# Seven block products instead of eight in three of eight pairs of the MLP's down product

## The chip, the cores and the metric

The kernel runs on one core of a Trainium2 chip. The metric is the time of one execution on the device in microseconds (us). The core has a matrix engine (TensorE, PE in the profile, with its weight loads as PEld), a vector engine (VectorE, DVE), a scalar engine (ScalarE, ACT), GpSimd (POOL) and SyncE (SP), which here only issues transfers. Each engine takes its instructions in a fixed order.

## The reference, cut to what matters

A two-layer trunk over 256 tokens of width 2048 in float32. Each layer mixes tokens (layer 0 by pooled means, layer 1 by dilated attention with 8 slots in 3 groups of heads) and then runs an MLP of width 8192:

```python
def sqrelu_mlp(x, w_up, w_down):
    h = jax.nn.relu(x @ w_up)
    return (h * h) @ w_down
...
    x = layer_norm(DEEPNORM_ALPHA * x + h, ln_mix_g[i], ln_mix_b[i])
    x = layer_norm(DEEPNORM_ALPHA * x + sqrelu_mlp(x, mlp_w_up[i], mlp_w_down[i]),
                   ln_mlp_g[i], ln_mlp_b[i])
```

## The kernel before, in words

**Split products.** A float32 matrix is held as a high and a low part in float32r. `split_from` (lines 61 to 63) makes them: ScalarE copies to the high part, VectorE subtracts it from the source. A product is three matmuls: high by high, high by low, low by high.

**Weights.** Weights come in chunks of 1024 elements for each of 128 partitions (512 KB), all listed in the order of use. `load` (line 116) fetches a chunk on SyncE's queue into one of 4 raw buffers; `prefetch` (line 129) splits it into one of 8 buffers of high and low parts. `weights()` (line 140) first splits up to 8 chunks ahead of the one in use, counting that one, and then hands it out. TensorE, VectorE and ScalarE run in the order in which the program writes their instructions. So a split that is issued after another operation on VectorE waits for that operation.

**An MLP.** `mlp` (line 520) cuts the 8192 hidden columns into four parts. For each part, `feature_major` forms the up product in blocks of 512 columns (8 chunks a block), hidden features on partitions. After each block `joined` adds two PSUM halves (lines 230, 231), `hidden` applies relu and square on ScalarE (lines 531, 533), and `split_hidden` makes `hH` and `hL`; these are eight pairs of row blocks of 128 for the down product. In the first part of a layer the first two blocks have 256 columns, and after each of the next four blocks `drain` restores a quarter of the residual `xz` on VectorE (lines 352, 353: four operations of 128x512, a multiply and an add for each of two token tiles). Then comes the down product. In three of the four parts (line 563) `token_major` takes 512 columns at a time and both tiles of 128 tokens: 16 row blocks, two tiles, three matmuls of 512 columns, which is 96 matmuls and 8 chunks; VectorE then adds two PSUM banks to `xz` (line 569 or 571). The fourth part goes through `closing`, which also makes the next norm. PSUM has 8 banks that are used in turn.

**Attention.** For each of four pairs of slots, after the third group's values, `transposes` (line 680) turns the weights of one slot with nine transposes, which ScalarE and VectorE split, and `values` multiplies. In the last three pairs `run_later` calls `values` right behind them.

Of the kernel before, what the change touches and what calls it, by code (L numbers as in the profile page):

```python
# [36 lines left out]
RESIDENT = 4  # L37
MLP_PARTS = 4
UP_FIRST = (256, 256, 512, 512, 512)
UP_REST = (512, 512, 512, 512)  # L40
# [6 lines left out]
def trunk(ctx: ExitStack, tc: tile.TileContext, x, pool_w_in, pool_w_group, pool_scale, pool_w_out,  # L47
# [28 lines left out]
    def plan(w, k0, nk, n0, ncols):  # L76
        step = CHUNK // ncols
        for k in range(k0, k0 + nk, step):
            chunks.append((w[:, k:k + step, n0:n0 + ncols], step, ncols))

    def plan_columns(w, k0, nk, n0, widths):
        for ncols in widths:
            plan(w, k0, nk, n0, ncols)
            n0 += ncols

    def plan_mlp(l):
        for c in range(MLP_PARTS):
            plan_columns(w_up[l], 0, KT, c * D, UP_FIRST if c == 0 else UP_REST)
            plan_columns(w_down[l], c * KT, KT, 0, CLOSING if c == MLP_PARTS - 1 else UP_REST)

# [3 lines left out]
    def plan_values(sp):  # L94

        w_v = w_qkv.rearrange("p k (y g n) -> p k y g n", y=3, g=GROUPS)
        for k in range(0, KT, 2):
            chunks.append((w_v[:, k:k + 2, 2, 1:3, sp * 256:(sp + 1) * 256], 2, 512))

# [11 lines left out]
    plan_mlp(1)  # L111

    raws, ready = [], []
    state = {"raw": 0, "split": 0, "used": 0}

    def load(upto):

        while state["raw"] < min(upto, len(chunks)):
            src, step, ncols = chunks[state["raw"]]
            raw = wraw.tile([P, step, ncols], F32, tag="raw", name="raw")  # L120
            if len(src.shape) == 4:
                for j in range(step):
                    nc.sync.dma_start(raw[:, j, :].rearrange("p (g n) -> p g n", g=src.shape[2]), src[:, j])
            else:
                nc.sync.dma_start(raw, src)
            raws.append(raw)
            state["raw"] += 1

    def prefetch(upto):

        while state["split"] < min(upto, len(chunks)):
            load(state["split"] + 1)
            _, step, ncols = chunks[state["split"]]
            hi = wsplit.tile([P, step, ncols], F32R, tag="wh", name="wh")
            lo = wsplit.tile([P, step, ncols], F32R, tag="wl", name="wl")
            split_from(hi, lo, raws.pop(0))
            ready.append((hi, lo))
            state["split"] += 1

    def weights(ahead=SPLITS):  # L140

        prefetch(state["used"] + max(ahead, 1))
        state["used"] += 1
        return ready.pop(0)

    def resident(n):

        prefetch(state["used"] + n)
        state["used"] += n
        return [ready.pop(0) for _ in range(n)]  # L150
# [114 lines left out]
    def tile_products(ps, t, nk, parts, act, start=True, between=()):  # L265

        k = 0
        for i, (hi, lo) in enumerate(parts):
# [7 lines left out]
            k += step  # L276


    class Norm:
        def __init__(self, g, b, cidx, last=None):  # L280
# [58 lines left out]
        def restores(self):  # L339
# [18 lines left out]
            return [lambda n=n: restore(n) for n in range(NG)]  # L358

        def centre(self, t, ns):  # L360
            for n in ns:
                z = xz[:, t, n * 512:(n + 1) * 512]
                nc.vector.scalar_tensor_tensor(z, z, self.mv[t][:, 0:1], self.last[:, 0, n * 512:(n + 1) * 512],
                                               op0=OP.subtract, op1=OP.mult)

        def output(self, t, ns):
            for n in ns:
                sl = slice(n * 512, (n + 1) * 512)
                z = xz[:, t, sl]
                nc.vector.scalar_tensor_tensor(z, z, self.r[t][:, 3:4], self.last[:, 1, sl],  # L370
                                               op0=OP.mult, op1=OP.add)
                nc.sync.dma_start(out[0, t * P:(t + 1) * P, sl], z)

    def closing(nk, act, first, norm, before_last=None):

        held = RESIDENT if norm.last is None else SPLITS
        nres = held * CHUNK // (nk * CLOSING[-1])
# [5 lines left out]
        per = nk * CLOSING[-1] // CHUNK  # L383
        prefetch(state["used"] + SPLITS)
        parts = resident(held)
        def tile_end(t, between=()):
            ps = []
# [13 lines left out]
        norm.moments(0)  # L401
        if norm.last is not None:
            norm.centre(0, [0])
# [32 lines left out]
    def opening(norm, ncols):  # L436
# [7 lines left out]
        for n in range(NG):  # L444
            norm.scaled(1, n)
            norm.features(1, n)
        prefetch(state["used"] + 2)
        tile_products(both[:, 1, :], 1, KT, parts, x_parts, start=False)
# [71 lines left out]
    def mlp(norm_in, norm):  # L520
        with ExitStack() as ph:
            hp = ph.enter_context(tc.tile_pool(name="hp", bufs=8))
            hb = ph.enter_context(tc.tile_pool(name="hb", bufs=2))
            if norm.last is not None:
                for i, v in enumerate((norm.g, norm.b)):
                    nc.gpsimd.dma_start(norm.last[:, i, :], v[None, :].to_broadcast([P, D]))

            def hidden(ps):
# [7 lines left out]
            def split_hidden(q):  # L536
# [3 lines left out]
                return hH, hL  # L540

            for c in range(MLP_PARTS):
                hs = []
                q0 = hidden(opening(norm_in, UP_FIRST[0])) if c == 0 else None
                for ncols in UP_FIRST[1:] if c == 0 else UP_REST:
# [16 lines left out]

                if c < MLP_PARTS - 1:
                    for n in range(NG):
                        ps = token_major(KT, 512, act)
                        for t in range(NT):
                            z = xz[:, t, n * 512:(n + 1) * 512]
                            if c == 0:
                                nc.vector.scalar_tensor_tensor(z, z, ALPHA, ps[t], op0=OP.mult, op1=OP.add)
                            else:  # L570
                                nc.vector.tensor_add(z, z, ps[t])
                else:
                    closing(KT, act, False, norm)
# [6 lines left out]
    with ExitStack() as ph:  # L580
# [44 lines left out]

        def project_values():
            ps = token_major(KT, 512, x_parts)
            hi, lo = value_pair()
# [79 lines left out]
        for sp in range(SLOTS // 2):  # L708
# [42 lines left out]

    fin = ctx.enter_context(tc.tile_pool(name="fin", bufs=1))
    last = fin.tile([P, 2, D], F32, name="last")
    mlp(norm2, Norm(ln_mlp_g[1], ln_mlp_b[1], None, last))


# [21 lines left out]
```

## Time and profile before

| | us |
|---|---|
| median of 3 runs | 2146.39 (2146.17 to 2149.98) |
| the profiled execution | 2146.52 |
| its span from the first to the last instruction | 2144.7 |
| TensorE busy | 2124.7 (99%) |
| VectorE busy | 1283.4 (60%) |
| ScalarE busy | 1052.8 (49%) |

Matmuls are pipelined, so the duration of one (377 ns in the mean at line 245) is longer than the distance from one to the next. The granted TensorE clock is 0.999 of full speed over the span.

### The profile page before, as it was taken

What the parts mean: (1) busy time and instruction counts of PE and PEld (TensorE: products, weight loads), DVE (VectorE), ACT (ScalarE), POOL (GpSimd) and SP (SyncE); (2) the same over time, 40 slices, a digit from 0 to 9 for tenths busy, and PEclk for the clock granted to TensorE, in tenths of its full rate; (3) what the DMA queues carried; (4) which work ended last, traced back from release to release, by engine and by line L of the source; (5) the groups of instructions that cost most, each with busy time, mean ns of one, the idle gap of its engine ahead of it and who ended that gap; (6) DMA issues with size and microseconds to landing.
All of it is one profiled execution on the core that took longest, in us unless ns stands there. A gap on an engine that the chain in (4) does not pass through costs nothing.

```text
span 2144.7 us, 29773 instructions
## 1 busy us (share of the span) xinstructions
PE 2124.7 (99%) x11745; PEld 1845.9 (86%) x11745; DVE 1283.4 (60%) x1558; ACT 1052.8 (49%) x1368; POOL 23.0 (1%) x52
## 2 busy tenths in 40 slices
PE   8999999999999999999999999999999999999998
PEld 7889888888888888898998988888888888888887
DVE  6785756555455555578656565676655555554555
ACT  4563655454355355354545444455545534644541
POOL 1000000000000000001000000000000000000000
PEclk9999999999999999999999999999999999999999
DMA  7565567556655655548555555456665566566562
GB/s 239 204 216 177 169 204 237 175 199 201 191 185 196 194 172 206 194 139 237 173 175 161 176 162 173 164 164 218 209 221 178 201 197 188 176 207 186 181 207 94
DMA packets 256045, 404.67 MB, mean 189 GB/s; under 512 B 13104, under 2 KB 109984, under 8 KB 255648
## 3 DMA queue, kind: packets, MB, share of 16 engines
q1 hardware_dynamic: 253472, 394.31, 56.7%
q0 software_dynamic: 2432, 8.45, 1.9%
q8 instruction: 92, 1.51, 0.3%
q14 instruction: 49, 0.40, 0.1%
HBM read 400.61 MB, written 2.10 MB: 188 GB/s over the span
## 4 chain that ended last, share of the span: by engine, by line
PE 96%; DVE 2%; DMA 1%; ACT 1%; issue 0%; SPq 0%; DVEq 0%; ACTq 0%
PE pt L245 45%; PE pf L202 32%; PE pf L204 16%; PE pf L221 1%; PE pq L658 1%; PE po L697 1%; DMA raw<-in_attn_w_qkv 0%; DVE wl L63 0%; PE ptr L321 0%; DMA xz<-in_x 0%; ACT xv L330 0%; DVE xT L337 0%; DVE vL L63 0%; PE ptr L458 0%; DVE xT L336 0%
## 5 line engine op out<-in xcount | busy, mean ns | idle before, releaser
L63 DVE TENSOR_TENSOR wl<-raw,wh 128x1024 fp32r<-128x1024 f32 x744 | 898.2, 1224 | 621.1 <-ACT wh L62 607.1
L62 ACT ACTIVATE wh<-raw 128x1024 fp32r<-128x1024 f32 x744 | 773.4, 1057 | 805.8 <-PE pt L245 351.4
L202 PE MATMUL pf<-xT,wh 128*128 128x512 f32 x3008 | 947.6, 396 | 0.0
L204 PEld LDWEIGHTS pf<-xT,wl 128*128 128x128 f32 x3008 | 566.0, 188 | 134.0 <-DVE wl L63 0.6
L204 PE MATMUL pf<-xT,wl 128*128 128x256 f32 x3008 | 592.2, 278 | 0.0
L202 PEld LDWEIGHTS pf<-xT,wh 128*128 128x128 f32 x3008 | 459.5, 189 | 0.5
L245 PE MATMUL pt<-wl,hH 128*128 128x512 f32 (+1 forms) x1088 | 407.0, 377 | 0.0
L245 PE MATMUL pt<-wh,hH 128*128 128x512 f32 (+1 forms) x1088 | 407.0, 377 | 0.0
L245 PE MATMUL pt<-wh,hL 128*128 128x512 f32 (+1 forms) x1088 | 398.2, 377 | 0.0
L245 PEld LDWEIGHTS pt<-wl,hH 128*128 128x128 f32 x1088 | 204.8, 188 | 37.6 <-DVE wl L63 0.4
L245 PEld LDWEIGHTS pt<-wh,hH 128*128 128x128 f32 x1088 | 204.8, 188 | 37.5
L245 PEld LDWEIGHTS pt<-wh,hL 128*128 128x128 f32 x1088 | 199.6, 188 | 37.1
L245 PE MATMUL pt<-wh,xT 128*128 128x256 f32 (+1 forms) x704 | 156.4, 314 | 1.9 <-DVE xT L336 1.5
L245 PEld LDWEIGHTS pt<-wh,xT 128*128 128x128 f32 x704 | 117.2, 191 | 10.6 <-DVE xT L336 3.1
L63 DVE TENSOR_TENSOR hL<-q,hH 128x512 fp32r<-128x512 f32 x62 | 42.9, 693 | 125.6 <-ACT hH L62 125.6
L245 PE MATMUL pt<-wl,xT 128*128 128x256 f32 (+1 forms) x352 | 106.7, 312 | 0.0
L230 ACT ACTIVATE low<-pf 128x256 f32<-128x256 f32 x188 | 61.3, 377 | 69.6 <-PE pf L204 62.7
L245 PE MATMUL pt<-wh,pT 128*128 128x512 f32 (+1 forms) x320 | 82.6, 347 | 0.0
L231 DVE TENSOR_TENSOR u<-pf,low 128x256 f32<-128x256 f32 x172 | 64.7, 418 | 26.0 <-ACT low L230 26.0
L245 PEld LDWEIGHTS pt<-wl,xT 128*128 128x128 f32 x352 | 67.2, 191 | 3.6
L531 ACT ACTIVATE r<-u 128x512 f32<-128x512 f32 x62 | 39.2, 632 | 51.0 <-DVE u L231 51.0
L245 PEld LDWEIGHTS pt<-wh,pT 128*128 128x128 f32 x320 | 56.1, 189 | 7.5
(126 smaller groups left out, 1001.8 us busy)
## 6 DMA issues: line engine op xcount, KB each, us to landing
raw<-in_mlp_w_up SPq DMA_DIRECT2D x256, 512.0 KB, 4.4
raw<-in_mlp_w_down SPq DMA_DIRECT2D x256, 512.0 KB, 4.5
raw<-in_attn_w_qkv SPq DMA_DIRECT2D x120, 512.0 KB, 4.3
raw<-in_pool_w_in SPq DMA_DIRECT2D x32, 512.0 KB, 5.4
raw<-in_pool_w_out SPq DMA_DIRECT2D x32, 512.0 KB, 4.7
raw<-in_attn_w_qkv SPq DMA_DIRECT2D x48, 256.0 KB, 3.3
raw<-in_attn_w_out SPq DMA_DIRECT2D x16, 512.0 KB, 4.4
raw<-in_pool_w_group SPq DMA_DIRECT2D x8, 512.0 KB, 5.0
```

Of the source, the lines that this page charges most:

```text
L62: nc.scalar.activation(hi, src, AF.Copy)
L63: nc.vector.tensor_sub(lo, src, hi.bitcast(F32))
L202: nc.tensor.matmul(ps[b], hi[:, j, sl], a, start=(k == 0), stop=False, skip_group_check=True)
L204: nc.tensor.matmul(ps[b][:, 0, :], lo[:, j, sl], a[:, 0, :], start=False, stop=(k == nk - 1), skip_group_check=True)
L221: nc.tensor.matmul(ps[b // 2][:, b % 2, :], w[:, j, sl], a[:, part, :], start=(k == 0 and i == 0 and b % 2 == 0), stop=(k == nk - 1 and i ...
L230: nc.scalar.activation(low, p[:, 1, :], AF.Copy)
L231: nc.vector.tensor_add(out[:, b, :], p[:, 0, :], low)
L245: nc.tensor.matmul(ps, a[:, sl], u, start=(start and k == 0 and i == 0), stop=(k == nk - 1 and i == 2), skip_group_check=True)
L531: nc.scalar.activation(r, ps, AF.Relu)
L658: nc.tensor.matmul(pq[:, t, :], q[u][:, b, sl], k[v][:, b, :], start=(i == 0), stop=(i == 2))
L697: nc.tensor.matmul(po, v[:, st, b * P:(b + 1) * P], p[:, g, sl], start=(i == 0), stop=(i == 3 * 2 * GROUPS - 1))
```

## The change

In the first three parts of each MLP the down product is formed for 1024 columns at a time by `mixed_group`. Of eight pairs of row blocks, taken in the order 1, 0, 3, 2, 5, 4, 6, 7, the pairs 1, 3 and 5 are treated as a product of 2x2 blocks (two token tiles by two row blocks, times two row blocks by two column halves) and formed by seven block products of sums and differences; the other pairs by eight. All eight banks of PSUM collect the products, and `sums` (8 VectorE operations) and four closing additions bring them into `xz`. The weight sums are made on VectorE in float32 and then split (`split_seven`), the sums of the hidden blocks likewise (`split_seven_left`). A seven-product chunk is two raw buffers and four split buffers, and `prefetch` counts it as four units of eight. Besides: plain chunks of these parts hold one row block by 1024 columns; in attention `transposes` moves ahead of the last value chunk in the last three pairs; the gain and bias rows of the last norm go into raw buffers on SyncE's queue at the last `closing`, and no longer through GpSimd's queue into a buffer of their own.

```diff
+MIX = (1, 0, 3, 2, 5, 4, 6, 7)
+SEVEN = (1, 3, 5)
+WIDE = 1024
...
+    def plan_mixed(w, k0, n0):
+        for i in MIX:
+            k = k0 + 2 * i
+            if i in SEVEN:
+                chunks.append((w[:, k:k + 2, n0:n0 + WIDE], 2, WIDE, 4))
+            else:
+                plan(w, k, 2, n0, WIDE)
...
+    def split_seven(a, b):
+        left, right = a[:, :512], a[:, 512:]
+        t = state["diff"].tile([P, 4, 512], F32, tag="t", name="t")
+        nc.vector.tensor_sub(t[:, 0], right, left)
+        nc.vector.tensor_sub(t[:, 1], b[:, :512], left)
+        nc.vector.tensor_add(t[:, 2], b[:, :512], t[:, 0])
+        nc.vector.tensor_sub(t[:, 3], b[:, 512:], t[:, 2])
+        parts = []
+        for src in (right[:, None, :], t[:, 0:2], b.rearrange("p (i n) -> p i n", i=2), t[:, 2:4]):
+            parts.append(split_buffers([P, 2, 512]))
+            split_from(parts[-1][0][:, :src.shape[1]], parts[-1][1][:, :src.shape[1]], src)
...
     def prefetch(upto):
-        while state["split"] < min(upto, len(chunks)):
+        while state["split"] < len(chunks) and begins[state["split"] + 1] <= upto:
...
+    def lookahead(n):
+        prefetch(begins[state["used"]] + n)
...
+    def mixed_group(act, left_factors, z, first):
+        names = ("P1", "P5", "P7", "P6", "P2", "P3", "P4", "P0")
+        ps = {name: bank([P, 512], "pt") for name in names}
...
+        def sums():
+            one, two, three = (tmp.tile([P, 512], F32, tag="xv", name="us", bufs=3) for _ in range(3))
+            nc.scalar.activation(one, ps["P1"], AF.Copy)
+            nc.vector.tensor_add(two, ps["P6"], one)
+            add(0, 1, ps["P1"], True)
+            nc.vector.tensor_add(three, ps["P7"], two)
+            nc.vector.tensor_add(two, ps["P5"], two)
+            add(1, 1, three, True)
+            nc.vector.tensor_add(three, ps["P5"], three)
+            add(0, 0, two, True)
+            add(1, 0, three, True)
+
+        last_seven = max(MIX.index(i) for i in SEVEN)
+        for n, i in enumerate(MIX):
+            a, b = 2 * i, 2 * i + 1
+            if i in SEVEN:
+                w, f = weights(), left_factors[i]
+                for name, left, right in (("P1", tokens(a, 0), "B11"), ("P5", f(0), "T1"), ("P7", f(2), "T3"),
+                                          ("P6", f(1), "T2"), ("P2", tokens(b, 0), "B21"), ("P3", f(3), "B22"),
+                                          ("P4", tokens(b, 1), "T4")):
+                    product(name, left, w[right], n == last_seven and name in ("P1", "P5", "P7", "P6"))
+            else:
+                for k in (a, b):
+                    hi, lo = weights()
+                    for name, t, h in (("P2", 0, 1), ("P3", 0, 0), ("P4", 1, 1), ("P0", 1, 0)):
+                        sl = slice(h * 512, (h + 1) * 512)
+                        product(name, tokens(k, t), (hi[:, 0, sl], lo[:, 0, sl]), n == len(MIX) - 1 and k == b)
+            if n == last_seven + 1:
+                sums()
+        add(0, 1, ps["P2"])
+        add(0, 0, ps["P3"])
+        add(1, 1, ps["P4"])
+        add(1, 0, ps["P0"])
...
+            def split_seven_left(q):
+                (a11, a21), (a12, a22) = ((q[:, i, :P], q[:, i, P:]) for i in range(2))
+                d = hb.tile([P, 4, P], F32, tag="r", name="d")
...
+                split_from(dH, dL, d)
...
-                        hs.append(split_hidden(hidden(u)))
+                        q = hidden(u)
+                        if c < MLP_PARTS - 1 and len(hs) in SEVEN:
+                            left_factors[len(hs)] = split_seven_left(q)
+                        hs.append(split_hidden(q))
...
-            vs.extend([project_value(pair, 1)] if sp == 0 else project_values())
-            transposes(sc[js[0]])
+            if sp == 0:
+                vs.append(project_value(pair, 1))
+                transposes(sc[js[0]])
+            else:
+                vs.extend(project_values(lambda: transposes(sc[js[0]])))
```

## Rows read from the trace of the kernel before

**Rows 1.** Page, part 1: busy us (share of the span), instructions.
```profile
PE 2124.7 (99%) x11745; PEld 1845.9 (86%) x11745; DVE 1283.4 (60%) x1558; ACT 1052.8 (49%) x1368; POOL 23.0 (1%) x52
```
**Rows 2.** Busy time by stretch: two down products, the up product between; header names columns.
```profile
core 0: us, PE busy (x) PEld busy (x) DVE busy (x) ACT busy (x) POOL busy (x), PEclk, DMA share, GB/s
308.50:395.80 87.30, 87.30 (x386) 72.00 (x385) 52.71 (x53) 42.66 (x46) 1.06 (x2) 1.00 0.72 238
395.80:485.00 89.20, 89.20 (x514) 77.88 (x513) 48.06 (x54) 48.24 (x64) 0.00 (x0) 1.00 0.57 187
485.00:572.05 87.05, 87.05 (x385) 72.10 (x385) 45.36 (x45) 37.84 (x40) 0.00 (x0) 1.00 0.62 196
```
**Rows 3.** Chain that ended last: three of six down products; start, length.
```profile
308.50 87.33 PE pt L245 x384
...
485.00 87.05 PE pt L245 x384
...
1517.13 87.11 PE pt L245 x384
```
**Rows 4.** Instruction groups by shape: busy us, mean ns, then idle before them.
```profile
L63 DVE TENSOR_TENSOR wl<-raw,wh 128x1024 fp32r<-128x1024 f32 x744 | 898.2, 1224 | 621.1 <-ACT wh L62 607.1 <-PE pf L204 6.5 <-PE pf L202 2.0
L62 ACT ACTIVATE wh<-raw 128x1024 fp32r<-128x1024 f32 x744 | 773.4, 1057 | 805.8 <-PE pt L245 351.4 <-PE pf L202 198.2 <-DMA raw<-in_mlp_w_down 111.3
...
L63 DVE TENSOR_TENSOR hL<-q,hH 128x512 fp32r<-128x512 f32 x62 | 42.9, 693 | 125.6 <-ACT hH L62 125.6
...
L661 DVE SCALAR_TENSOR_TENSOR sc<-dist,pq 128x128 f32<-128x128 f32 x24 | 6.7, 280 | 0.0
```
**Rows 5.** VectorE's timeline, first parts' down products: start, length (merged), idle before.
```profile
302.13 4.62 DVE L63 TENSOR_TENSOR wl<-raw,wh 128x1024 fp32r<-128x1024 f32 x4
311.96 5.19 DVE L63 TENSOR_TENSOR wl<-raw,wh 128x1024 fp32r<-128x1024 f32 x4 [5.20 <-ACT wh L62]
317.06 0.75 DVE L231 TENSOR_TENSOR u<-pf,low 128x256 f32<-128x256 f32 x2
...
323.23 0.69 DVE L63 TENSOR_TENSOR hL<-q,hH 128x512 fp32r<-128x512 f32 x1 [2.03 <-ACT hH L62]
323.83 0.69 DVE L352 TENSOR_TENSOR xz<-xz,gb 128x512 f32<-128x512 f32 x1
...
326.49 4.62 DVE L63 TENSOR_TENSOR wl<-raw,wh 128x1024 fp32r<-128x1024 f32 x4
...
1534.86 4.63 DVE L63 TENSOR_TENSOR wl<-raw,wh 128x1024 fp32r<-128x1024 f32 x4
```
**Rows 6.** TensorE's timeline at the eighth chunk of that product.
```profile
327.41 0.39 PE L245 MATMUL pt<-wh,hH 128*128 128x512 f32 x1
327.76 0.50 PE L245 MATMUL pt<-wl,hH 128*128 128x512 f32 x1
```
**Rows 7.** VectorE's timeline, second part's down product: its last hidden block, then weights.
```profile
484.64 0.76 DVE L231 TENSOR_TENSOR u<-pf,low 128x256 f32<-128x256 f32 x2 [0.30 <-ACT low L230]
...
490.80 0.69 DVE L63 TENSOR_TENSOR hL<-q,hH 128x512 fp32r<-128x512 f32 x1 [2.02 <-ACT hH L62]
491.75 4.63 DVE L63 TENSOR_TENSOR wl<-raw,wh 128x1024 fp32r<-128x1024 f32 x4 [0.26 <-ACT wh L62]
...
506.53 1.28 DVE L571 TENSOR_TENSOR xz<-xz,pt 128x512 f32<-128x512 f32 x2
```
**Rows 8.** Page, part 6: transfers, KB each, median us from issue to landing.
```profile
raw<-in_mlp_w_down SPq DMA_DIRECT2D x256, 512.0 KB, 4.5
```
**Rows 9.** TensorE's timeline in attention: the last transpose, the third value matmul.
```profile
1147.89 0.27 PE L685 MATMUL pp<-ident,sc 128*128 128x128 f32 x1
...
1149.06 0.39 PE L697 MATMUL po<-PTL,vH 128*128 128x256 f32 x1 [0.30 <-DVE PTL L63]
```
**Rows 10.** Busy time by stretch at the end; columns as in rows 2.
```profile
2134.00:2135.00 1.00, 0.15 (x2) 0.00 (x0) 0.78 (x2) 0.00 (x0) 0.00 (x0) 1.00 0.00 0
...
2139.00:2140.00 1.00, 0.00 (x0) 0.00 (x0) 1.00 (x3) 0.00 (x0) 0.00 (x0) 0.61 0.00 0
```

More of the change, by code (lines that the diff above doesn't have):

```diff
@@ L111, in trunk @@
     plan_mlp(1)
+    begins = [0]
+    for c in chunks:
+        begins.append(begins[-1] + c[3])
     raws, ready = [], []
@@ L118, in load @@
         while state["raw"] < min(upto, len(chunks)):
-            src, step, ncols = chunks[state["raw"]]
-            raw = wraw.tile([P, step, ncols], F32, tag="raw", name="raw")
-            if len(src.shape) == 4:
+            src, step, ncols, units = chunks[state["raw"]]
+            if units > 1:
+                raw = [wraw.tile([P, ncols], F32, tag="raw", name="raw") for _ in range(step)]
                 for j in range(step):
-                    nc.sync.dma_start(raw[:, j, :].rearrange("p (g n) -> p g n", g=src.shape[2]), src[:, j])
+                    nc.sync.dma_start(raw[j], src[:, j])
@@ L124, in load, with split_buffers @@
             else:
-                nc.sync.dma_start(raw, src)
+                raw = wraw.tile([P, step, ncols], F32, tag="raw", name="raw")
+                if len(src.shape) == 4:
+                    for j in range(step):
+                        nc.sync.dma_start(raw[:, j, :].rearrange("p (g n) -> p g n", g=src.shape[2]), src[:, j])
+                else:
+                    nc.sync.dma_start(raw, src)
             raws.append(raw)
             state["raw"] += 1
+    def split_buffers(shape):
+        return [wsplit.tile(shape, F32R, tag="w" + x, name="w" + x) for x in "hl"]
@@ new lines, in split_seven @@
+    def split_seven(a, b):
[9 more added lines that the diff above has]
+            split_from(parts[-1][0][:, :src.shape[1]], parts[-1][1][:, :src.shape[1]], src)
+        (one, diff, low, sums) = parts
+        return {name: (h[:, i], l[:, i]) for name, (h, l), i in (
+            ("B11", one, 0), ("T1", diff, 0), ("T3", diff, 1), ("B22", low, 0), ("B21", low, 1),
+            ("T2", sums, 0), ("T4", sums, 1))}
@@ L129, in prefetch @@
     def prefetch(upto):
-        while state["split"] < min(upto, len(chunks)):
+        while state["split"] < len(chunks) and begins[state["split"] + 1] <= upto:
             load(state["split"] + 1)
[L133 to L137, printed above, removed]
+            _, step, ncols, units = chunks[state["split"]]
+            raw = raws.pop(0)
+            if units > 1:
+                ready.append(split_seven(*raw))
+            else:
+                hi, lo = split_buffers([P, step, ncols])
+                split_from(hi, lo, raw)
+                ready.append((hi, lo))
@@ L146, in resident @@
     def resident(n):
[L148 removed]
+        lookahead(n)
         state["used"] += n
@@ L358, in restores, with rows_of_last, row @@
             return [lambda n=n: restore(n) for n in range(NG)]
+        def rows_of_last(self):
+            self.rows = []
+            for v in (self.g, self.b):
+                for n0 in range(0, D, CHUNK):
+                    self.rows.append(wraw.tile([P, CHUNK], F32, tag="raw", name="row"))
+                    nc.sync.dma_start(self.rows[-1], v[None, n0:n0 + CHUNK].to_broadcast([P, CHUNK]))
+        def row(self, i, n):
+            return self.rows[i * D // CHUNK + n // 2][:, n % 2 * 512:(n % 2 + 1) * 512]
         def centre(self, t, ns):
@@ L374, in closing @@
     def closing(nk, act, first, norm, before_last=None):
-        held = RESIDENT if norm.last is None else SPLITS
+        held = RESIDENT if not norm.last else SPLITS
         nres = held * CHUNK // (nk * CLOSING[-1])
@@ L401, in closing @@
         norm.moments(0)
-        if norm.last is not None:
+        if norm.last:
             norm.centre(0, [0])
@@ L563, in mlp @@
                 if c < MLP_PARTS - 1:
[L564 to L571, printed above, removed]
+                    for n0 in range(0, D, WIDE):
+                        mixed_group(act, left_factors,
+                                    lambda t, h: xz[:, t, n0 + h * 512:n0 + (h + 1) * 512], c == 0)
                 else:
```

61 lines of the change are left out of this document (43 added, 18 removed).

## The prediction

> **What bounds the kernel now.** I read the page's busy shares first: TensorE 99% of a span of 2144.7 us, VectorE 60% [rows 1]. That is an average, so next came the busy time by stage. The six stretches that change are the three down products of each layer that end in a plain addition: 384 matmuls in 87.05 us [rows 3], 0.2267 us each from start to start, with no gap. In such a stretch VectorE is busy 45.4 us, or 52.7 us in the first of a layer [rows 2]. The forecast hangs on VectorE's timeline where a down product begins, and that is where the reader should look: just after that start VectorE spends 6.9 us on the last hidden block (317.06 to 323.92), 2.7 us on restoring the residual (323.83 to 326.49), and only then splits weights again [rows 5]. The eighth weight chunk of the down product is the first of that burst. It is ready at about 327.72 (326.49 and one 1.23 us subtraction) and TensorE, which wants it at 308.50 + 7 x 2.72 = 327.5, starts its second product at 327.76 instead of 327.64 [rows 6]. So at this place the first part of a layer has no reserve at all; in the other layer the same burst starts at 1534.86 [rows 5] and the product at 1517.13 [rows 3], 17.7 us on instead of 18.0, again with almost nothing spare.
>
> **The change on TensorE.** A pair of row blocks was 24 matmuls for 1024 columns and becomes 21. Three pairs, two column halves, six parts: 3 x 3 x 2 x 6 = 108 matmuls fewer, all on the path, 108 x 0.2267 = 24.5 us saved. A seven-product pair then takes 4.76 us, a plain one 5.44, a part 83.0 instead of 87.05.
>
> **The change on VectorE.** A 1024-wide weight subtraction lasts 1.22 us alone and follows the one before by (4.62 - 1.23)/3 = 1.13 us [rows 4, 5]; two 512-wide additions from PSUM take 1.28 us together, 0.6 us apart [rows 7]; four 512-wide ones in SBUF take the 2.66 us of the restore [rows 5]. A seven-product chunk was two subtractions (2.3 us). It becomes four 512-wide sums (2.66) and splits of 0.6 + 3 x 1.13 (4.0): 6.7 us. ScalarE's part, 3.5 x 1.06 = 3.7 us [rows 4], lies beside it. The sums of block products add eight 512-wide operations to each of 12 groups, 5.3 us each. By stage: six such chunks add 26 us to a part and two sums 10.6, so VectorE's 45.4 becomes 82 against TensorE's 83.0, and the 52.7 of a first part becomes 90. VectorE sets the pace there. Each left factor (pairs 1, 3, 5) adds four 128-wide operations, at 0.28 us by the nearest row, and a 512-wide subtraction of 0.69 [rows 4]: 1.8 us in the chain of its hidden block. Nothing covers it, for VectorE waits there for ScalarE, which waits for it.
>
> [...]
>
> **How a down product begins.** Eight units of split weights are kept ahead. Before, seven chunks (19 us of TensorE) were split ahead of the last hidden block. Now a seven-product chunk takes four units, and only the first of them and two plain chunks are ahead: 4.76 + 5.44 = 10.2 us. The second one, B, comes behind the hidden block in VectorE's program order.
>
> *Second and third parts* (four of the six). The hidden block ends at 491.49 - 485.00 = 6.5 us [rows 3, 7]. B's last split is ready at 6.5 + 6.7 = 13.2; TensorE wants it at 10.2 + 2.27 (P1, P5, P7 and one matmul) = 12.5: a stall of 0.7. From there VectorE has, up to the first of the closing additions that free PSUM banks, 2.3 (two chunks), 6.7, 6.8 (six chunks), 5.3 (sums), 6.7 (the next group's first chunk), 2.3, 0.65: it ends at 44.0 without waits, and at up to 47 if weights that land 4.5 us after their issue [rows 8] arrive late at two places, since VectorE now holds the four raw buffers longer. TensorE wants that bank at 41.5 + 0.7 + 2.7 = 44.9. That stall is 0 to 2 us; I take 1.0. Sum 1.75, bounds 0 and 4, four times: +7.0.
>
> *First parts* (two). Three left factors put the chain, which paces VectorE between bursts, 5.5 us later: the burst of 302.13 begins at 307.6. Its chunk was needed at 308.50 - 2.79 = 305.7 (a chunk of the up product is 89.2/32 [rows 2]), so TensorE stalls 3 us already there. Then 1.2 (that chunk), 6.7 (A) and 2.3: hidden block at 317.8, restore at 324.7, B's sums from 327.3, its last split at 334.0. TensorE finishes B 2.5 us later, at 336.5, against 308.50 + 4.76 + 5.44 + 4.76 = 323.5 with no stall: 13.0 us. With 0 to 1.6 for the bank (0.8 taken) 13.8, twice: +27.6. Bounds: 7 if the left factors cost nothing (B 5.5 us earlier, no late bank), 16 if the loads add to it.
>
> **Other edits.** In three of four head pairs transposes move ahead of the last value chunk, a chunk that covers their splits. TensorE now waits some 1149.06 - (1147.89 + 0.11) - 2 x 0.12 = 0.8 us there [rows 9], 0.11 and 0.12 being half the pace of 0.2267 for matmuls of at most 256 columns; behind them the value splits still come late, so I take 0.5 gained, bounds 0 and 0.8: -1.5. Plain chunks of one row block and 1024 columns move the same bytes and feed the same 12 matmuls: 0. The last norm's rows go from two transfers on GpSimd's queue to four on SyncE's, 512 KB each, behind the last weights and ahead of the output's. They are wanted only after the first tile's closing products, 48 x 0.2267 = 10.9 us, which cover 4.5 us of landing [rows 8]; uncovered they would cost those 4.5.
>
> **Sum.** -24.5 - 1.5 + 7.0 + 27.6 = +8.6. The profiled execution took 2146.5 us (span 2144.7 and 1.8 around it), beside a median of 2146.4: 2155.1 us.
>
> **Rivals.**
> (1) *VectorE keeps ahead.* If the splits of B were done before they are wanted, only the saving is left: 2146.5 - 26 = 2120.5, faster. For it: the share of VectorE over the whole span stays near 71%. Against: order on VectorE is the program's, the reserve of 10.2 us is shorter than hidden block plus B (13.2), and the row at 327.76 shows no slack.
> (2) *The left factors are absorbed.* Fewer chunks are split before the hidden block now, so the wait for loads inside the burst (306.7 to 312.0 [rows 5]) goes. If this also takes up the 5.5 us, a first part stalls 7.5 us: -26 + 15 + 7 = -4, 2142.5 us, on the edge of faster. The sign turns at a stall of (26 - 7)/2 = 9.5 us in a first part. Against: that wait is already left out of my walk.
> [...]
>
> **How the numbers follow.** A measurement here can tell about 0.2%, 4.3 us. My forecast has 0.55, its own range 2148 to 2163 us; of it 0.38 lies above 2150.7 and 0.17 within 0.2%. Rival 1 has 0.12, rival 2 0.16 (half faster, half same), rival 3 0.17 (slower). Together: faster 0.20, same 0.25, slower 0.55. From 2134 to 2168 about 0.8 is held: rival 1 and half of rival 3 lie outside.
>
> **What would show it.** Right: in 308 to 400 and 1517 to 1610 the stretch of down products is longer than 87 us, about 97, with VectorE busy some nine tenths and TensorE waiting for it at the start; in the other four it is 84 to 86 us, with first waits some 13 us in; matmuls fall by 108, and VectorE's busy time rises by some 250 us (36 x 4.4 + 12 x 5.3 + 18 x 1.8). Wrong: first parts of 83 to 90 us, or the four others over 88. The step that I trust least is the 13 us of a first part, since one order of work on VectorE makes it.

## The result, and the profile after

The changed kernel took 2170.48 us in the median of four runs (2169.10 to 2171.14), the kernel before 2146.28 in four runs beside it: a ratio of 1.0108 (95% interval 1.0090 to 1.0125; it is worked out from the single runs, the two medians alone give 1.0113). It is slower, as forecast, but by 23.5 us between the two profiled executions (2146.52 and 2169.97) where 8.6 were said, and above the range of 2148 to 2163. The page of the profile, part 1, and then the busy time by stretch of the six down products, with the columns of [rows 2]:

```profile
PE 2118.3 (98%) x11637; PEld 1831.6 (84%) x11637; DVE 1511.0 (70%) x1960; ACT 1117.5 (52%) x1470; POOL 22.0 (1%) x50
```
```profile
311.71:405.79 94.08, 86.32 (x368) 69.70 (x368) 81.54 (x98) 51.68 (x60) 1.06 (x2) 0.98 0.62 206
494.95:580.06 85.11, 83.57 (x369) 68.52 (x367) 73.28 (x89) 48.27 (x56) 0.00 (x0) 1.00 0.58 193
669.22:755.57 86.35, 83.61 (x368) 68.47 (x367) 73.95 (x89) 48.65 (x56) 0.00 (x0) 1.00 0.56 190
1528.07:1625.30 97.23, 89.62 (x368) 71.23 (x367) 83.59 (x101) 52.87 (x61) 0.00 (x0) 0.95 0.59 198
1714.47:1802.51 88.04, 85.30 (x368) 69.57 (x367) 76.00 (x91) 48.60 (x56) 0.00 (x0) 0.98 0.58 192
1891.67:1980.12 88.45, 85.45 (x368) 69.59 (x367) 74.85 (x90) 48.49 (x56) 0.00 (x0) 0.98 0.56 187
```

The 108 matmuls are gone and VectorE has 227.6 us more to do, against [rows 1]. With no stall each stretch would be 83.0 us. The four stretches of second and third parts are 2.1, 3.4, 5.0 and 5.5 us longer, 16.0 in all where 7.0 were said; those of layer 1 are the ones with a mean clock of 0.98, and both are over the 88 us that the prediction named as a sign against it. The first parts begin late as well: from the second up block (256 columns) to the end of the down product layer 0 takes 176.1 us (229.66 to 405.79) and layer 1 179.8 (1445.53 to 1625.30), where 165.8 and 165.6 less 4.1 saved were possible: 14.4 and 18.3 us lost, 32.7 in all where 27.6 were said.

What TensorE waited for, over the whole span (us in total, times, longest):

```profile
PE pt L343 <- DVE xz L355: 11.0, 6, 2.1
PE pt L343 <- DVE wl L67: 8.4, 11, 2.2
PE pt L343 <- DVE u L285: 5.9, 4, 1.9
...
PE pf L258 <- DVE wl L67: 5.3, 3, 2.9
```

The first row is one wait in each of the six parts, in the middle: in the second group's first chunk the fifth product wants a bank that a closing addition (line 355) has not yet read. The other three belong to the first parts for the most part: the late up chunk (line 258), the banks of the last up block, which VectorE adds late (line 285), and B, the second seven-product chunk of a group (A is the first). In the second and third parts the wait for B is 0.6 us each, where 0.7 was said. VectorE's timeline at the first down product, beside [rows 5]:

```profile
306.71 1.22 DVE L67 TENSOR_TENSOR wl<-raw,wh 128x1024 fp32r<-128x1024 f32 x1
...
316.65 0.75 DVE L285 TENSOR_TENSOR u<-pf,low 128x256 f32<-128x256 f32 x2
...
323.42 0.68 DVE L465 TENSOR_TENSOR xz<-xz,gb 128x512 f32<-128x512 f32 x1
...
326.08 0.69 DVE L163 TENSOR_TENSOR t<-raw 128x512 f32<-128x512 f32 x1
...
331.48 1.22 DVE L67 TENSOR_TENSOR wl<-t,wh 128x1024 fp32r<-128x1024 f32 x1
```

The walk of the forecast put these at 307.6 (the late chunk), 317.8 (hidden block), 324.7 (restore), 327.3 (B's sums) and 334.0 (B's last split ready; here 332.7). It held within 1.3 us.

What the walk did not hold is the clock. Busy time in 1 us stretches around the bank wait of layer 1's second part; the granted clock is the third column from the end:

```profile
1758.00:1760.00 2.00, 1.87 (x8) 1.05 (x7) 2.00 (x2) 1.35 (x2) 0.00 (x0) 1.00 0.54 182
1760.00:1761.00 1.00, 0.00 (x0) 0.00 (x0) 1.00 (x2) 0.00 (x0) 0.00 (x0) 1.00 0.61 234
1761.00:1762.00 1.00, 0.00 (x0) 0.00 (x1) 1.00 (x3) 0.00 (x0) 0.00 (x0) 1.00 0.70 188
1762.00:1763.00 1.00, 1.00 (x4) 0.86 (x5) 1.00 (x2) 0.00 (x0) 0.00 (x0) 0.97 0.88 299
1763.00:1764.00 1.00, 1.00 (x4) 0.71 (x4) 1.00 (x3) 0.00 (x0) 0.00 (x0) 0.50 0.59 152
1764.00:1765.00 1.00, 1.00 (x4) 0.81 (x3) 1.00 (x3) 0.00 (x0) 0.00 (x0) 0.50 0.69 233
1765.00:1766.00 1.00, 1.00 (x4) 0.81 (x3) 0.97 (x2) 0.94 (x1) 0.00 (x0) 0.50 0.46 188
1766.00:1767.00 1.00, 1.00 (x5) 0.79 (x4) 1.00 (x3) 1.00 (x3) 0.00 (x0) 0.82 0.00 0
```

TensorE stands still for 2 us and runs for 1, and then the granted clock reads 0.50 for 3 us. The column lacks 0.03 + 3 x 0.50 + 0.18, so 1.7 us of full clock are lost. There are seven such falls of 1.7 us each, two at the start of each first part and three at bank waits, all of these in layer 1.

### The profile page after: what moved, and what is told of

The parts are those of the page before. It is cut to its first block, busy times and chain, and to the rows that moved or that the text cites. A ratio compares the mean times of both kernels' runs of the same rounds, so it can differ in the third digit from the quotient of the medians.

```text
span 2168.2 us, 30026 instructions
## 1 busy us (share of the span) xinstructions
PE 2118.3 (98%) x11637; PEld 1831.6 (84%) x11637; DVE 1511.0 (70%) x1960; ACT 1117.5 (52%) x1470; POOL 22.0 (1%) x50
## 4 chain that ended last, share of the span: by engine, by line
PE 75%; DVE 14%; DMA 5%; ACT 3%; issue 2%; DVEq 0%; SPq 0%; ACTq 0%
PE pf L256 28%; PE pt L299 21%; PE pf L258 14%; PE pt L343 11%; DVE wl L67 6%; DMA raw<-in_mlp_w_down 3%; DMA raw<-in_mlp_w_up 1%; ACT wh L66 1%; DMA raw<-in_pool_w_in 1%; PE pq L793 1%; PE po L832 1%; DVE xz L355 1%; DVE u L285 1%; DVE win L624 1%; DVE t L166 1%
## 5 line engine op out<-in xcount | busy, mean ns | idle before, releaser
L67 DVE TENSOR_TENSOR wl<-raw,wh 128x1024 fp32r<-128x1024 f32 (+1 forms) x744 | 875.4, 1196 | 402.4 <-ACT wh L66 397.2
L66 ACT ACTIVATE wh<-raw 128x1024 fp32r<-128x1024 f32 (+1 forms) x744 | 757.7, 1035 | 602.1 <-PE pf L256 162.5
L343 PE MATMUL pt<-wh,hH 128*128 128x512 f32 x588 | 232.0, 395 | 16.9 <-DVE xz L355 11.0
L343 PE MATMUL pt<-wl,hH 128*128 128x512 f32 x588 | 231.1, 393 | 4.7 <-DVE wl L67 4.7
L343 PE MATMUL pt<-wh,hL 128*128 128x512 f32 x588 | 230.5, 392 | 0.0
L343 PEld LDWEIGHTS pt<-wh,hH 128*128 128x128 f32 x588 | 111.6, 190 | 44.4 <-DVE xz L355 13.6
L343 PEld LDWEIGHTS pt<-wl,hH 128*128 128x128 f32 x588 | 111.7, 190 | 28.5 <-DVE wl L67 5.9
L299 PE MATMUL pt<-wh,hH 128*128 128x512 f32 (+1 forms) x320 | 107.9, 347 | 0.0
L299 PE MATMUL pt<-wl,hH 128*128 128x512 f32 (+1 forms) x320 | 107.8, 347 | 0.0
L299 PE MATMUL pt<-wh,hL 128*128 128x512 f32 (+1 forms) x320 | 99.2, 347 | 0.0
```

The costliest lines, as they stand in the source:

```text
L66: nc.scalar.activation(hi, src, AF.Copy)
L67: nc.vector.tensor_sub(lo, src, hi.bitcast(F32))
L299: nc.tensor.matmul(ps, a[:, sl], u, start=(start and k == 0 and i == 0), stop=(k == nk - 1 and i == 2), skip_group_check=True)
L343: nc.tensor.matmul(ps[name], a[u], w[v], start=(name not in begun), stop=(last and i == 2), skip_group_check=True)
```

## The experiments

Ratios are to the kernel before, whose median beside them was 2147.2 to 2147.4 us; differences between experiments are those of their medians. The changed kernel was not run again beside them, and the kernel before was 1.0 us faster beside it than beside them, so a difference of a microsecond or two from the changed kernel says nothing.

**Which part pays: e1 and e2.** Seven products in the second and third parts alone, and in none.

```diff
-    def plan_mixed(w, k0, n0):
+    def plan_mixed(w, k0, n0, seven):
...
-            if i in SEVEN:
+            if i in seven:
...
-plan_mixed(w_down[l], c * KT, n0)
+plan_mixed(w_down[l], c * KT, n0, SEVEN if c in PARTS else ())   # e1: PARTS = (1, 2); e2: ()
```


> Seven-product pairs only in the second and third parts; the first part of each layer goes back to eight products per pair (in 1024-column groups, without left factors). Theory A (order: too little weight split ahead of the last hidden block, worst where the residual is restored too): the first parts cost +10.3 and +14.2 us by the stage marks of the two traces, so this gives 2170.5 - 24.5 = 2146 us, and the other four parts stay at 85 to 88.5 us each. Rival B (VectorE is simply full and its total work is what is lost, wherever it lies): two of six parts' work taken off, one third of the loss and of the saving, some 2162 us.

> Eight products in every pair, with all that came beside the seven products kept (1024-column groups and chunks, transposes ahead of the last value chunk, last norm's rows through raw buffers). Theory A: 2145 to 2146 us, half a microsecond to one and a half below the kernel before. Rival D (the wider chunks or the rows of the last norm carry a part of the loss): above 2150.

e1: 2146.94 us (ratio 0.9996, 0.9986 to 1.0006). e2: 2145.31 (0.9990, 0.9981 to 0.9999). Both are what the theory of order expected. The other edits of the change cost nothing; second and third parts break even, and the first parts make the loss.

**The bank wait: e3 and e7.** In plain chunks of a group the lookahead is cut so that the closing additions come ahead of the splits of the two plain chunks behind the next A. e7 does this with seven products in the second and third parts alone.

```diff
+        limit = begins[state["used"]] + 22 + 4
...
-                    hi, lo = weights()
+                    hi, lo = weights(min(SPLITS, limit - begins[state["used"]]))
```


> All work kept; only the order on VectorE and ScalarE changes at the end of each group: the four closing additions, which free PSUM banks, come ahead of the splits of the two plain chunks behind the next group's first seven-product chunk. Theory A: the bank waits at the middle of each part (1 to 2 us, six times) go, and with them three stretches of lower clock of 1.7 us each: 2155 to 2161 us. Rival B: VectorE has the same work, 2168 to 2171. Rival C (the clock costs nothing, TensorE would have waited anyway): 2159 to 2163.

> The first and the third of these runs together: seven products in second and third parts only, closing additions ahead of the splits. Theory A: each of four parts gains 4.1 us on TensorE and waits 0.7 us for the second seven-product chunk, so 2146 - 13 = 2132 to 2134 us, faster than both kernels. Rival B: 2144 to 2148.

e3: 2157.36 (1.0046, 1.0031 to 1.0061), 13.1 us less than the changed kernel; no wait for those additions is left among its waits. e7: 2138.08 (0.9957, 0.9942 to 0.9972), faster than both kernels, though each of its four parts gains 2.2 us on e1 where 3 and more were expected: a miss, between the ranges of both theories.

**The clock: e4 and e9.** Eight products with a zero left factor, which change no sum, go ahead of the first product that meets the bank wait, so that TensorE has work there; e9 adds such filler at three places at the start of the first parts.

```diff
+                    if second and n == 0 and name == "P2":
+                        idle_products(ps["P1"], w["B11"][0], 8)
+                    if first and not second and n == 0 and name in ("P2", "P4"):   # e9 as well
+                        idle_products(ps["P1"], w["B11"][0], 6)
+                    if first and not second and n == 2 and name == "P1":             # e9 as well
+                        idle_products(ps["P0"], last_w, 8)
...
```


> Work added to TensorE alone: in the second group of each part eight matmuls with a zero left factor (1.8 us, they add nothing) stand ahead of the product that waits for a bank, so TensorE is busy where it waited. Theory A: the clock no longer falls behind that wait (three of six parts, 1.7 us each) and the filler fits into the wait: 2164 to 2167 us. Rival C (the lower clock costs nothing because VectorE is behind anyway): 2169 to 2172.

> The same filler, and in the first part of each layer filler in the first group too: six zero matmuls ahead of each of two bank waits in the first seven-product chunk, eight ahead of the second one's first product. There VectorE is still behind when the clock falls, so theory A has little left to gain: 0 to 3 us below the run with filler at the middle alone, 2162 to 2167. If the clock's whole 1.7 us were lost at each fall there, 5 us below it: 2160.

e4: 2164.07 (1.0078, 1.0065 to 1.0091). Eight more matmuls at six places made the kernel 6.4 us faster; by the two traces all of it was gained in layer 1, where the three falls had been. The same bank wait in e4, columns as before:

```profile
1760.00:1761.00 1.00, 1.00 (x6) 0.78 (x5) 1.00 (x3) 0.00 (x0) 0.00 (x0) 1.00 0.65 234
...
1763.00:1764.00 1.00, 1.00 (x6) 0.84 (x5) 1.00 (x3) 1.00 (x3) 0.00 (x0) 1.00 0.07 16
```

So the falls at the bank waits are real losses: three of 1.7 us are 5.1 of the 6.4. e9: 2163.82 (1.0076, 1.0062 to 1.0090). Filling the starts as well brings nothing, although the full clock lost there shrinks from 8.5 us in e4 to 3.4: there TensorE has to wait for VectorE anyway, at either clock.

**The start of a first part: e8, e5, e5b.** e8 forms the left factors once in a layer and uses them for all pairs and parts of it, so that 16 of the 18 formations are left out (not 17, as the expectations say) and the product is no longer that of the reference: e8, and e15 and e16 below, tell of the time alone. e5 moves the restoring operation that stands between the last hidden block and B behind the sums of the first group; e5b does that on e3.

```diff
-                            left_factors[len(hs)] = split_seven_left(q)
+                            left_factors[len(hs)] = state["left"] = state.get("left") or split_seven_left(q)   # e8
...
-                    drain()                                  # e5, e5b
+                    if not (c == 0 and len(hs) == 8):
+                        drain()
...
                 sums()
+                drain()
```


> The left factors (sums of hidden blocks and their split) are formed once and used again in all later pairs, so 17 of 18 formations are left out and the products are not those of the reference. Theory A: in each first part the chain of hidden blocks and restores comes 3 x 1.83 = 5.5 us earlier (one formation less in the first layer), the other parts hardly change; with one fall of the clock less in the first layer 2157 to 2161 us. The rival of the prediction that the 5.5 us are absorbed by a shorter wait for loads: 2168 to 2171.

> The changed kernel (2170.5 us) with the restoring operation alone moved behind the sums of the first group. The queue theory gives up to 5 us and perhaps a fall of the clock less: 2164 to 2168 us. The theory of a full VectorE gives no change, since the bank wait between the groups takes back what B gained: 2169 to 2172 us.

> e3 (2157.4 us) with the restoring operation that stands between the last hidden block and B in the two first parts taken to the place behind the sums of the first group. If what makes B late is VectorE's queue ahead of it, this brings up to 2.7 us in each first part: 2152 to 2155 us. If VectorE is short of time over the whole first part, the moved operation makes a later split or sum late by as much: 2156 to 2159 us.

All three miss what the theory of a late queue expected. e8: 2165.75 (1.0087, 1.0074 to 1.0101), a gain of 4.7 us, between its two theories. e5: 2174.19 (1.0128, 1.0113 to 1.0144), above both of its ranges, and e5b: 2157.23 (1.0048, 1.0034 to 1.0061), where a VectorE short of time was expected: no gain. In e5 B's sums begin 2.2 us sooner, at 323.88, and the next chunk's then wait 0.65 us for a weight transfer.

**Another engine, another order: e10, e11, e12.** e10 puts the four weight sums of a chunk on GpSimd, on e3. e11 starts each group with a plain pair, so that more of TensorE's work lies ahead of A and B, and gives the banks out to match; e12 is e11 in the second and third parts alone.

```diff
-        nc.vector.tensor_sub(t[:, 0], right, left)
+        nc.gpsimd.tensor_sub(t[:, 0], right, left)      # e10: and the three sums below it
...
-MIX = (1, 0, 3, 2, 5, 4, 6, 7)
+MIX = (0, 1, 2, 3, 4, 5, 6, 7)                          # e11, e12
...
-        names = ("P1", "P5", "P7", "P6", "P2", "P3", "P4", "P0")
+        names = ("P2", "P3", "P4", "P0", "P1", "P5", "P7", "P6")
+        if second:
+            names = names[4:] + names[:4]
```


> Closing additions first, and the four float32 sums of each seven-product chunk made on GpSimd instead of VectorE (36 x 2.6 us less on VectorE). Theory A: the second chunk of each part is split some 2.6 us earlier if GpSimd makes the sums while VectorE is in the hidden block, so the wait of 0.7 us in four parts goes and each first part gains 3 to 5 us: 2142 to 2150 us, against 2157.4 with closing additions first alone. If GpSimd takes longer than some 6 us for the four, or slows VectorE: 2157 or more.

> All three parts keep seven products, and the closing additions keep their place of e3 (2157.4 us). The order inside each group becomes plain pair, A, plain, B, plain, C, plain, plain, and the banks are named so that the first plain products of a first group take banks that the last up block does not hold, and those of a second group the banks that the sums have freed. No instruction is added or removed. Theory of the reserve: at the entry of a first part the eight split buffers then cover 5.4 + 4.8 + 5.4 = 15.6 us of TensorE's work in place of 10.2, so the wait for B shrinks by about 5 us in each of the two first parts, and the bank wait between the groups goes too, since a plain pair lies ahead of A: 2143 to 2148 us. Rival: VectorE is full from the last up blocks to the end of a first part, so that a different order only moves the wait from B to C or to the end: 2155 to 2158 us.

> The order and the banks of e11 with seven products in the second and third parts alone, as in e7 (2138.1 us). In those parts VectorE has time, so what is left of waits there should be the order's: the reserve theory gives 2132 to 2136 us. The rival, that what e7 still lacked of 3.4 us a part is VectorE's own time in these parts, gives 2137 to 2139 us.

e10: 2163.40 (1.0072, 1.0058 to 1.0086), 6.0 us slower than e3: the gain that was hoped for is missed, and what the expectation named for a slow GpSimd came. Groups of instructions of e10, GpSimd's and VectorE's (busy, mean ns, idle before):

```profile
L164 POOL TENSOR_TENSOR t<-raw 128x512 f32<-128x512 f32 x36 | 64.5, 1793 | 16.5 <-DMA raw<-in_mlp_w_down 16.4
...
L163 POOL TENSOR_TENSOR t<-raw 128x512 f32<-128x512 f32 x36 | 61.5, 1707 | 620.4 <-DMA raw<-in_mlp_w_down 521.1 <-DVE wl L67 83.5 <-ACT hH L66 15.9
```
```profile
L67 DVE TENSOR_TENSOR wl<-raw,wh 128x512 fp32r<-128x512 f32 x36 | 40.7, 1131 | 0.2 <-ACT wh L66 0.2
```

A sum takes 1.6 to 1.8 us there, and the 512-wide subtraction that VectorE makes of such a chunk 1131 ns in the mean, against 685 in the changed kernel. Single instructions of e10 show that it depends on what lies beside them (start, length):

```profile
360.78 0.68 DVE L67 TENSOR_TENSOR wl<-raw,wh 128x512 fp32r<-128x512 f32 x1
...
538.18 2.47 DVE L356 TENSOR_TENSOR xz<-xz,pt 128x512 f32<-128x512 f32 x4
538.52 1.30 POOL L163 TENSOR_TENSOR t<-raw 128x512 f32<-128x512 f32 x1 [5.43 <-DMA raw<-in_mlp_w_down]
...
542.89 2.28 POOL L165 TENSOR_TENSOR t<-raw,t 128x512 f32<-128x512 f32 x1
543.94 1.78 DVE L67 TENSOR_TENSOR wl<-raw,wh 128x512 fp32r<-128x512 f32 x1
```

With no GpSimd sum beside it the subtraction takes 0.68 us, beside one 1.78; four closing additions, whose second input is a PSUM bank, take 2.47 us together, 0.6 us apart, also beside one (676 ns each in the mean of e10, 678 in the changed kernel).

e11: 2172.73 (1.0117, 1.0103 to 1.0131), 15.4 us slower than e3; both theories miss. e12: 2138.12 (0.9958, 0.9946 to 0.9971), as e7 and in the range of its rival: its down products do shrink to 83.0 to 83.5 us, but the next up block then waits 1.3 us in the mean for a bank that the sums hold. VectorE's timeline in e11 shows what the order ran into:

```profile
310.54 0.69 DVE L163 TENSOR_TENSOR t<-raw 128x512 f32<-128x512 f32 x1
316.23 0.69 DVE L164 TENSOR_TENSOR t<-raw 128x512 f32<-128x512 f32 x1 [5.01 <-DMA raw<-in_mlp_w_down]
```

VectorE, late already, stands for 5.0 us inside A for A's second raw row. The four raw buffers were taken, so that row could not be fetched sooner.

**Less work ahead of a first part: e13, e14, e15.** Restoring operations one by one earlier, in the up blocks: on the changed kernel, on e3, and on e3 with the left factors formed once.

```diff
                         hs.append(split_hidden(q))
+                        if c == 0 and len(ps) == 4 and i == 0:
+                            drain()
                     drain()
```


> The changed kernel (2170.5 us) with the four restoring operations of each layer put one up block pair after another, so that the last two stand before the last up block instead of inside it and behind it. The same instructions, 5.4 us of VectorE's work per first part moved to a stretch in which VectorE is busy for two thirds of the time. If VectorE's work between the last up block and the end of the first part sets the time, each first part gains 5 us and a part of its clock falls: 2156 to 2161 us. If the loads into the raw buffers set it, only the wait for the late up chunk (2.0 and 2.9 us) goes, or is given back: 2166 to 2171 us.

> The same edit on e3 (2157.4 us), where the closing additions stand ahead of the splits for later plain chunks. VectorE's work as the cause: 2144 to 2149 us. Loads as the cause: 2153 to 2158 us.

> The kernel of e14 in which a layer forms its left factors for one block pair alone and uses them for all (17 of 18 formings of 5.4 us on VectorE left out in every two layers, so the product is not the reference's). With the restoring operations and the left factors both gone from the entry, the theory of VectorE's work expects first parts that cost no more than plain ones or gain like the others, 2135 to 2142 us, against 2144 to 2149 of e14. The theory of the loads expects 2150 us or more here too.

e13: 2169.07 (1.0102, 1.0086 to 1.0118). e14: 2157.93 (1.0049, 1.0037 to 1.0062). e15: 2156.28 (1.0039, 1.0026 to 1.0052). All three lie where the theory of the loads put them. None gains more than 1.7 us over its base, so with four raw buffers VectorE's work at that place is not by itself what sets the time. (By its timeline e14 takes one restoring operation out of the crowded stretch, not two: one stays ahead of the late chunk.) What does set it shows in the up blocks ahead. VectorE's timeline of the changed kernel there, then SyncE's queue, then the busy time of 301 to 307:

```profile
280.92 4.62 DVE L67 TENSOR_TENSOR wl<-raw,wh 128x1024 fp32r<-128x1024 f32 x4
290.49 5.22 DVE L67 TENSOR_TENSOR wl<-raw,wh 128x1024 fp32r<-128x1024 f32 x4 [4.95 <-ACT wh L66]
295.63 0.75 DVE L285 TENSOR_TENSOR u<-pf,low 128x256 f32<-128x256 f32 x2
```
```profile
293.12 1.67 SPq L144 DMA_DIRECT2D raw<-in_mlp_w_down  x2
295.74 12.54 SPq L151 DMA_DIRECT2D raw<-in_mlp_w_down  x2
311.09 2.60 SPq L144 DMA_DIRECT2D raw<-in_mlp_w_down  x2
```
```profile
301.00:307.00 6.00, 4.98 (x29) 4.01 (x27) 5.08 (x11) 2.71 (x5) 0.00 (x0) 1.00 0.00 0
```

VectorE splits four chunks, waits 4.95 us for ScalarE's copy, which waits for a transfer, splits four more, and only then comes to the hidden pairs. While it works on these (from 295.6 on) all four raw buffers are full and nothing is fetched: from 301 to 307 the transfers move 0 GB/s. What is taken out of VectorE's queue comes back as a wait for the next load.

**More raw buffers: e16, e17, e18.** In the MLP the raw chunks go round a ring of five buffers in e17 (on e14; the sums `u` of the up blocks give the room), of six in e16 (on e15; the room of left factors that are not kept), and of five in the kernel before (e18).

```diff
-                        u = hb.tile([P, 2, S], F32, tag="u", name="u")
+                        u = tmp.tile([P, 2, S], F32, tag="xv", name="u", bufs=3)   # e17
...
+    def raw_tile(shape):
+        if state["raw"] < state["extra_end"]:
+            state["turn"] += 1
+            if state["turn"] % (RAWS + 1) >= RAWS:      # e16: RAWS + 2
+                return state["extra"].tile(shape, F32, tag="raw", name="raw")
+        return wraw.tile(shape, F32, tag="raw", name="raw")
```


> The kernel of e15 (2156.3 us; 17 of 18 formings of left factors left out, so the product is not the reference's) with two more raw buffers in the MLP, which come out of the room of the left factors not kept: a ring of six in place of four, used by every up and down weight there. If the loop of load, split and release through the raw buffers makes VectorE late, the idle 5 us inside the up blocks go, the wait for the late up chunk goes, and each first part gains 3 to 6 us: 2144 to 2150 us. If VectorE's queue from the last up block on is the limit by itself, nothing changes: 2154 to 2158 us.

> The kernel of e14 (2157.9 us, everything formed) with one more raw buffer in the MLP, its room gained by letting the sums u of the up blocks use the buffers of the transposed rows. The loop theory expects half to all of what six buffers bring: 2149 to 2154 us. The theory of VectorE's queue expects 2156 to 2159 us.

> The kernel before (2147.4 us) with the same ring of five raw buffers in the MLP. TensorE waits only 3 us in all in its down parts, so both theories expect 2145 to 2148 us; a gain beyond that would say that part of what a ring brings in the other kernels is no cost of the change.

e17: 2141.70 (0.9974, 0.9964 to 0.9985), 16.2 us below e14 by one buffer of 512 KB, with all parts formed by seven and faster than the kernel before. In e17 the sums `u` also go round three buffers in place of two, which no run tells apart; e16 leaves them as they were. e18: 2146.36 (0.9996, 0.9987 to 1.0005): there the buffer is worth nothing. e16: 2129.89 (0.9916, 0.9902 to 0.9929), 26.4 us below e15 by two buffers. The gains of e17 and e16 are larger than expected. Busy time by stretch in layer 0: the three 512-column up blocks of the first part in e14 and in e17, then the down products of first and second parts in e17 and in e16:

```profile
241.34:316.01 74.67, 70.28 (x388) 60.26 (x387) 51.11 (x75) 37.62 (x54) 4.25 (x8) 0.96 0.62 186
```
```profile
240.85:309.54 68.69, 67.54 (x388) 58.44 (x386) 48.59 (x72) 35.19 (x52) 4.27 (x8) 1.00 0.63 200
309.54:399.84 90.30, 86.28 (x368) 68.99 (x367) 81.27 (x98) 52.09 (x61) 0.00 (x0) 0.98 0.64 207
489.01:572.91 83.90, 83.30 (x368) 68.56 (x367) 74.53 (x91) 47.84 (x56) 0.00 (x0) 1.00 0.61 197
```
```profile
308.31:393.41 85.10, 83.91 (x369) 68.47 (x368) 76.09 (x92) 47.75 (x56) 0.00 (x0) 1.00 0.63 212
482.57:566.45 83.88, 83.27 (x368) 68.58 (x367) 74.82 (x91) 47.71 (x56) 0.00 (x0) 1.00 0.59 201
```

The same three up blocks take 66.98 us in the kernel before. Most of what the fifth buffer brings lies there, where the last chunk of these blocks is split at 305.81 us and no longer at 310.29: 6.0 us in layer 0, and 6.6 in layer 1 by the same stretch.

And VectorE's waits from the up blocks to the end of the first down product, in e14 and in e17:

```profile
DVE wl L67 <- ACT wh L66: 25.1, 16, 5.1
```
```profile
DVE wl L67 <- ACT wh L66: 15.9, 9, 4.1
```

The copies on ScalarE that VectorE waits for wait themselves for the loads: 40.7 us in that stretch of e14 (27.3 for up weights, 13.4 for down weights), 27.9 in e17. VectorE executes 1960 instructions in both.

In the changed kernel the same gap repeats, 4.77 and 4.95 us in which VectorE is idle in two successive up blocks, and e17 and e16 show the cause. The gap alone does not say what it costs: in the kernel before it is as long ([rows 5]: 5.20 us) and the fifth buffer brings nothing (e18), and in e17 3.71 and 4.12 us of it are left.

## Why the prediction missed its size

**TensorE's saving and the other edits** were right: 108 matmuls fewer, and e2 within 0.1% of the kernel before. Between the two MLPs the change gained 0.4 us (7.48 us behind at 844.74, 7.04 at 1445.53) where 1.5 were taken. So of the 14.9 us missed 1.1 lie there, 9.0 in second and third parts (16.0 for 7.0) and 5.1 in first parts (32.7 for 27.6); the rest of the kernel gives 0.3 back.

**The step that is missing is the one about the clock.** The sum has no term for it. It fell seven times, around pauses of 1.8 to 2.2 us. Three of these falls stand at the bank waits in the middle of a part, and there they cost 6.4 us (e4; 5.1 by the granted clock). The four at the starts of first parts cost next to nothing (e9: 2163.82 us against the 2164.07 of e4). The one fall in the rows of the kernel before follows a stop of 5 us at its end [rows 10]; what a shorter one does they could not show.

**The term that was too small is the wait for a bank**: 1.0 us taken in four parts and 0.8 in two, 5.6 in all, and 11.0 measured. Clock and bank wait together are 11.8 of the 14.9 us missed, and moving the closing additions alone gave back 13.1 (e3). With the 1.1 of the attention 2 us are left, which no run splits.

**The start of a first part** was right in what waits and when, and in layer 0 in size: 14.4 us lost against 13.8. The 18.3 of layer 1 hold three falls of the clock instead of two (1.7 us more), and the wait for the late up chunk is 2.92 us there against 2.00; the rest of the difference is open. The reason that the walk gave is not borne out, and so its size is in part luck. It blamed the left factors (5.5 us each time) and the restore for B's lateness, and taking these away brought 4.7 us at most while four raw buffers set the pace (e8, e13 to e15). It came out near the truth all the same because it began from VectorE's times in the kernel before, in which the waits for loads in the up blocks (4.72 and 4.91 us, 4.77 and 4.95 after) were already contained.

**The loads** were in the bounds ("if the loads add to it", "arrive late at two places") and not in the sum. They cost 16.2 us (e17 against e14): by the traces 12.6 in the up blocks of first parts and some 1.1 in each of the four other parts. Falls of the clock that go with late weights are in that figure: the first parts lose 8.5 us of full clock in e14 and 1.7 in e17. On the changed kernel itself, with its bank waits, a fifth buffer was not run. With the loads out of the way the left factors do show: e16, without them and with a sixth buffer, is 11.8 us faster than e17, about the 11 us said of them. The two causes are not told apart in that figure.

**The rivals.** Rival 3 had 0.17 of the 0.55 for slower, and slower it came, above the range. Among the causes that the runs show are the clock's falls at the bank waits (6.4 us, e4) and the loads (16.2 us, e17 against e14); in the first parts the falls have no price (e9). Rival 1, VectorE keeping ahead, is what e16 comes near to (2129.9 against 2120.5). Rival 2 is not borne out in its time, for a first part lost 14.4 us and more where it had 7.5. Its mechanism is in part: without the left factors the changed kernel gains 4.7 us and not 11 (e8), so the wait for loads takes up the rest of what removing them would give.

## What to carry to other kernels

When an edit gives an engine more work per transfer, look at how long that engine now holds each landing buffer: here one more raw buffer was worth 16 us, and taking 5 to 11 us of work out of the same engine's queue at the suspected place 5 us at most. Count a short wait of TensorE with the clock that may fall behind it (1.7 us of full clock each time here), and put the operations that free its banks ahead of work for later. Seven products pay where VectorE has time left: 2138.1 us with the first parts left plain (e7). e7 with five raw buffers was not run; from 83.9 us a stretch in e17 against 87.05 it should come to about 2146.5 - 4 x 3.15 - 0.4 = 2133.5 us, an estimate.

## What the runs showed of the hardware that was not expected

The clock can fall around a pause of 2 us, and doesn't always. Three waits of TensorE in the changed kernel:

```profile
716.65 0.50 PE L343 MATMUL pt<-wh,hH 128*128 128x512 f32 x1 [2.13 <-DVE xz L355]
...
1525.64 0.50 PE L258 MATMUL pf<-xT,wl 128*128 128x256 f32 x2 [2.92 <-DVE wl L67]
...
1762.00 0.51 PE L343 MATMUL pt<-wh,hH 128*128 128x512 f32 x1 [2.13 <-DVE xz L355]
```

Behind the first two the granted clock stayed at 1.00 in each microsecond, up to 730 and up to 1533; behind the third, a pause as long as the first, it fell. What decides it, these runs do not show. Matmuls with a zero factor held it up in e4, at a gain of 6.4 us. And GpSimd's operations stretched VectorE's subtraction of two SBUF operands from 0.68 to 1.78 us beside them in e10, and not its additions from a PSUM bank (676 ns in the mean there, 678 in the changed kernel).
